# A two-layer mixture-of-experts encoder on one core: layer 1's gather in two float32r parts, and the sums of a block in halves at other places

## The chip, the core and the metric

The kernel runs on one core of a Trainium2 chip. Its engines are TensorE (PE, with its weight loads as PEld), VectorE (DVE), ScalarE (ACT), GpSimd (POOL) and SyncE (SP), which issues the loads from memory. The metric is the device time of one execution in microseconds; lower is better.

## What is computed

Two layers over 256 tokens of width 1024, each a token mixer (windowed attention, a state-space part and latent attention, joined by an output projection) followed by experts, and one normalisation at the end. The change lies in the experts. Each token picks one of 4 groups and 2 of its 8 experts (32 in all), each with matrices of 1024 x 256 (gate, up) and 256 x 1024 (down), all in float32:

```
for g in range(N_EXPERT_GROUPS):
    h = jax.nn.silu(jnp.einsum('nd,edf->enf', xt, w_gate[g])) * jnp.einsum('nd,edf->enf', xt, w_up[g])
    h = h * gate[:, g].T[:, :, None].astype(h.dtype)
    y = y + jnp.einsum('enf,efd->nd', h, w_down[g])
```

Only the tokens that chose an expert have a gate other than zero, and the kernel computes each expert for those alone.

## The kernel before

**Blocks.** `ORDER` (L26) puts the experts of a layer into nine blocks, of two experts with up to 64 token slots each or of four with 32. In layer 1 these are, in order: 16-17, 0-3, 18-19, 4-7, 8-11, 12-15, 20-23, 24-27, 28-31. Neighbouring blocks of equal size and consecutive experts form a group (L1206): in layer 1, 4-7 with 8-11 and 20-23 with 24-27; the others stand alone. A block has 128 slots, so a group has 128 or 256.

**Gather.** `onehot` (L1214) makes a 0/1 matrix `P` that takes tokens to the slots of a group, in two halves of 128 tokens. `gather` (L1232), for each of 8 slices `k` of the width, multiplies the normalised tokens `xn` (the stationary operand, 128 x 128) by `P` (moving, 128 or 256 columns), both halves of tokens into one bank, and ScalarE or VectorE in turn moves the result with the gain into the page `xe`. The first group is gathered at the layer's start, any other during the last block of the group before it, slices 0 to 3 and 4 to 7 apart (L1578 to L1585). `xn` is written by `normed` (L1175), a ScalarE copy of the tokens times their scale, at the end of the mixer (steps `r0` and `r1` of `SEQ`).

**A block** (from L1518): `fill_slots` turns the weighted one-hot into the combine matrix `Sm`; `gate_up` (L1440) multiplies the gathered slots by the gate and up weights, in two halves of the width; `hidden` (L1345) is a ScalarE silu and a VectorE product, `hidden_t` (L1351) two transposes and a copy; `down` (L1459) multiplies by the down weights, and `split_y` (L1359) splits the result into two float32r parts. `combine` (L1245) adds the block to the tokens `x`, for each half of the width and of the tokens by two float32r matmuls (L1251, L1252) and a VectorE addition (L1253). It is done late: the sums of a block are pending (`pend`) until the next block's gate products are through. The order in the program is: gate products of both halves; then for part 0 and 1: the next group's gather of that part, the pending sum of that part, and after part 0 the transposes of `hidden_t`; then an `If` (L1598) that all engines pass; then the down products.

```
for part in range(2):
    if ib == nb - 1 and nxt:
        for k in range(4 * part, 4 * part + 4):
            gather(nxt[0], nxt[1], k)
    if pend is not None:
        combine(pend, (part,))
    if part == 0:
        hT = hidden_t(hh)
```

**Overflow.** With more than 32 tokens for an expert of a block of four, `second` (L1489, under the `If`s of L1568 and L1598) repeats the block for the rest, with a gather of its own (`gather_all`, L1477); with more than 64 or 128, `unit` (L1381) does 128 slots of one expert, after the sixth block of layer 1 (`UNIT_AT`). Its gather (L1398) moves 512 columns of `xn`. In the profiled execution one unit and one `second` run, both in layer 1.

**Order on the engines.** The tile framework plans each engine's order at build time from the program order and from what its plan has ready; `pin` keeps a few in place. An `If` is planned as a unit.

**Loads.** Weights come in pages of 1 MB (128 x 8 KB) through one SP queue in the order of `chunks`. The ring has `NPAGE` = 25 pages, shared by weights and work pages. `room` (L211) lets a page in as long as weights and work pages fit, with `st["peak"]` pages kept for work; `done` and `work_done` free pages and call `pump` (L227), which issues the next loads. `KEEP` (L42), the pages `xe` and `xn`, is held from `r0` to the end of a layer's experts.

Of the kernel before, what the change touches and what calls it, by code (L numbers as in the profile page):

```python
# [41 lines left out]
KEEP = ("xe", "xn")  # L42
# [7 lines left out]
        "gl": ("ub", "qkv", "hT", "hTl"), "R": (), "r0": KEEP, "r1": KEEP, "e0": KEEP, "e1": KEEP, "h0": (), "h1": (), "k0": (), "k1": (),  # L50
# [111 lines left out]
def hybrid_encoder_kernel(ctx, tc, I, out, dbg=None):  # L162
# [48 lines left out]
    def room(key):  # L211
# [13 lines left out]
        return key in eat or len(KEEP) + sum(1 for k in st["tiles"] if k not in eat) < NPAGE  # L225
# [339 lines left out]
    def uses(l, w):  # L565
# [8 lines left out]
        if w in USES:  # L574
            u = list(USES[w])
        elif w[0] in "nq":
# [38 lines left out]
    def mixer(l):  # L615
# [68 lines left out]
        with tc.tile_pool(name=f"mx{l}", bufs=1, reuse_waits="tile") as mp:  # L684
# [413 lines left out]
            next(follow(l, SEQ[l].split() + ["|"], steps, KEEP))  # L1098
            st["plan"], st["peak"] = None, len(KEEP)
# [3 lines left out]
    class Router:  # L1103
# [22 lines left out]
        def pages(self):  # L1126

            self.xe = work["xe"]
            self.xT, self.xn = page_sm(self.xe, 0, (8, T)), page_sm(work["xn"], 0, (2, 8, 128))
            self.junk = self.xn[:, 1].rearrange("p k d -> p (k d)")  # L1130
# [44 lines left out]
        def normed(self, tt):  # L1175
            S.activation(self.xn[:, tt], self.xk[:, tt], AF.Copy, scale=self.r2[:, tt:tt + 1])
# [17 lines left out]
    def moe(l, tab, rt):  # L1194
        with tc.tile_pool(name=f"moe{l}", bufs=1, reuse_waits="tile") as mo:
# [4 lines left out]

            xe_pg, xn, msk, rk, gate = rt.xe, rt.xn, rt.msk, rt.rk, rt.gate
            io32 = iota[:, 0:NE]
            st["peak"] = len(KEEP)
# [21 lines left out]
            def weigh(P, ex):  # L1225
                shape = [128, 2] + list(P.shape[2:])
                pgt = mt(shape, "pgt")
                G.tensor_tensor(pgt, P,  # L1228
# [152 lines left out]
            def unit(u):  # L1381
# [7 lines left out]
                Pu, Pg = mt([128, 2, 128], "Pu", tag="oh"), page_sm(scr[0], 1536, (2, 128))  # L1389
# [99 lines left out]
            def second(blk, w, hf):  # L1489

                if hf == 0:
                    sh = [128, 2, 4, 32]
                    e0 = blk[0]
                    P, Pg = w["P"], scr[0][:, 1280:1536].rearrange("p (t e c) -> p t e c", t=2, e=4)
# [211 lines left out]
```

## Time and profile before

| | us |
|---|---|
| median of 3 runs (727.12 to 731.55) | 730.94 |
| the profiled execution, its own time | 735.1 |
| its span, first to last instruction | 733.3 |
| PE busy | 639.2 (87%) |
| DVE busy | 373.2 (51%) |
| ACT busy | 252.9 (34%) |
| POOL busy | 107.4 (15%) |
| read from memory | 233.82 MB, 320 GB/s over the span |

Busy time is the time in which an engine has an instruction under way; PE's is modelled and runs over the drain of a matmul. An f32 matmul leaves two records, a float32r matmul one. "DVEq L1598" is VectorE's sequencer at the `If` of that line.

### The profile page before, as it was taken

How to read it: one execution, taken by the hardware profiler on the slowest of the kernel's cores; microseconds unless marked ns; L12 is line 12 of the kernel's file. 1: busy time of each engine (PE TensorE's matmuls, PEld its weight loads, DVE VectorE, ACT ScalarE, POOL GpSimd, SP SyncE). 2: the span in 40 equal slices, each digit the busy share in tenths (PEclk: the TensorE clock that was granted, in tenths of full speed). 3: DMA queues.
4: the chain of work that ended last, by engine and by line, in shares of the span. 5: the costliest groups of instructions: out<-in, count | busy, mean ns of one | idle time of the engine just before them, and what ended most of it. 6: DMA issues, size and time to landing. Idle time of an engine off the chain costs nothing. (4 is left out here: it accounts for less than half of the span.)

```text
span 733.3 us, 12000 instructions
## 1 busy us (share of the span) xinstructions
PE 639.2 (87%) x4370; PEld 389.2 (53%) x4370; DVE 373.2 (51%) x899; ACT 252.9 (34%) x578; POOL 107.4 (15%) x135
## 2 busy tenths in 40 slices
PE   7997989988799797778899899999989978889994
PEld 6584877744245243326468777775534434334442
DVE  3899977532432228624369877762333323422424
ACT  3647764332111113444073397432202111011113
POOL 1202000100000022312032754500000000000001
PEclk9999999999899999789999899997999999999998
DMA  8920374895999999999996714796799999999991
GB/s 309 419 105 0 118 275 177 329 386 200 409 410 416 307 416 407 414 414 409 396 417 251 286 59 142 261 363 267 241 414 408 413 408 415 412 410 358 408 380 71
DMA packets 57201, 232.82 MB, mean 317 GB/s; under 512 B 6049, under 2 KB 8481, under 8 KB 48161
## 3 DMA queue, kind: packets, MB, share of 16 engines
q1 hardware_dynamic: 57120, 231.75, 81.3%
q8 instruction: 51, 0.84, 0.5%
q14 instruction: 30, 0.24, 0.1%
HBM read 233.82 MB, written 1.05 MB: 320 GB/s over the span
## 5 line engine op out<-in xcount | busy, mean ns | idle before, releaser
L1451 PE MATMUL gu<-pg,xe 128*32 128x512 f32 (+1 forms) x1024 | 149.5, 619 | 11.4 <-DMA pg<-in_w_up_dram 9.9
L1467 PE MATMUL yp<-pg,scr 128*32 128x512 f32 (+2 forms) x560 | 77.9, 628 | 26.1 <-DVEq L1598 12.8
L1451 PEld LDWEIGHTS gu<-pg,xe 128*32 128x32 f32 (+1 forms) x1024 | 45.9, 117 | 98.8 <-issue 94.5
L1236 PE MATMUL gp<-oh,xn 128*128 128x128 f32 (+1 forms) x416 | 73.6, 331 | 3.9 <-DVE oh L1221 1.6
L1236 PEld LDWEIGHTS gp<-oh,xn 128*128 128x128 f32 x416 | 62.9, 201 | 19.0 <-issue 11.3
L1467 PEld LDWEIGHTS yp<-pg,scr 128*32 128x32 f32 (+1 forms) x560 | 21.6, 119 | 72.1 <-issue 57.2
L1361 DVE TENSOR_TENSOR y<-yp,y 128x512 fp32r<-128x512 f32 (+1 forms) x39 | 26.3, 677 | 65.2 <-ACT y L1360 65.2
L1253 DVE TENSOR_TENSOR x<-cp,x 128x512 f32<-128x512 f32 x76 | 48.9, 684 | 19.0 <-PE cp L1252 19.0
L1228 POOL TENSOR_TENSOR pgt<-oh,gate 128x256 f32<-128x256 f32 (+1 forms) x13 | 10.2, 782 | 305.5 <-PE slp L372 294.3
L1348 DVE SCALAR_TENSOR_TENSOR scr<-gu,gs,scr 128x256 f32<-128x256 f32 x19 | 9.2, 482 | 89.9 <-ACT scr L1347 89.9
L1360 ACT CAST y<-yp 128x512 fp32r<-128x512 f32 (+1 forms) x39 | 22.3, 574 | 86.5 <-PE yp L1467 82.7
L359 DVE TENSOR_SCALAR xe<-gp,vec 128x128 f32<-128x128 f32 (+1 forms) x52 | 20.8, 400 | 54.6 <-PE gp L1236 54.6
L355 ACT ACTIVATE xe<-gp,vec 128x128 f32<-128x128 f32 (+1 forms) x52 | 21.1, 408 | 76.5 <-PE gp L1236 76.5
L1347 ACT ACTIVATE scr<-gu 128x256 f32<-128x256 f32 x19 | 7.3, 383 | 99.8 <-PEq L1568 50.9
L1251 PE MATMUL cp<-y,sm 128*128 128x512 f32 x76 | 33.5, 449 | 0.3 <-PEq L1568 0.2
L1252 PE MATMUL cp<-y,sm 128*128 128x512 f32 x76 | 29.9, 402 | 1.5 <-DVE y L1361 1.5
L1058 DVE SCALAR_TENSOR_TENSOR x<-op,rg,x 128x512 f32<-128x512 f32 x24 | 17.9, 748 | 16.9 <-PE op L681 11.9
L1341 ACT ACTIVATE scr<-slp 128x256 f32<-128x256 f32 x20 | 7.7, 387 | 35.4 <-PE slp L372 15.6
L1251 PEld LDWEIGHTS cp<-y,sm 128*128 128x128 f32 x76 | 14.3, 189 | 10.4 <-issue 8.2
L372 PE MATMUL hp<-cst,scr 128*128 128x128 f32 x40 | 9.2, 313 | 10.9 <-DVE scr L1348 9.8
L548 PE MATMUL t4p<-ca,tabs 128*32 128x32 f32 (+3 forms) x512 | 16.3, 250 | 2.1 <-issue 2.1
L548 PEld LDWEIGHTS t4p<-ca,tabs 128*32 128x32 f32 x512 | 15.4, 116 | 3.3 <-issue 3.0
(454 smaller groups left out, 1210.2 us busy)
## 6 DMA issues: line engine op xcount, KB each, us to landing
pg<-in_w_gate_dram SPq DMA_DIRECT2D x128, 512.0 KB, 10.2
pg<-in_w_up_dram SPq DMA_DIRECT2D x128, 512.0 KB, 10.2
pg<-in_w_down_dram SPq DMA_DIRECT2D x56, 1024.0 KB, 12.0
pg<-in_w_o_dram SPq DMA_DIRECT2D x8, 1024.0 KB, 17.9
pg<-in_w_down_dram SPq DMA_DIRECT2D x12, 512.0 KB, 10.4
pg<-in_w_qk_dram SPq DMA_DIRECT2D x4, 1024.0 KB, 14.9
pg<-in_w_nat_dram SPq DMA_DIRECT2D x4, 960.0 KB, 12.9
wgu<-in_w_gate_dram SPq DMA_DIRECT2D x4, 512.0 KB
```

The costliest lines, as they stand in the source:

```text
L355: S.copy(dst, src) if scale is None else S.activation(dst, src, AF.Copy, scale=scale)
L359: e.tensor_scalar(dst, src, scale, None, op0=OP.mult)
L548: PE.matmul(t4p[b][32 * jq:32 * jq + 32, c + lo:c + hi], g0[ri][:, 8 * d + i, :], ca[ri][:, 8 * d + i, m, :].rearrange("p m c -> p (m c)") ...
L1058: V.scalar_tensor_tensor(xh, p, rg[:, g, tt:tt + 1], xh, op0=OP.mult, op1=OP.add)
L1236: PE.matmul(p[:, :w], xn[:, tt, k, :], P[:, tt].rearrange("p e c -> p (e c)"), start=(tt == 0), stop=(tt == 1))
L1251: PE.matmul(p, Sm[:, 128 * tt:128 * tt + 128], yh[:, c], start=True, stop=False)
L1252: PE.matmul(p, Sm[:, 128 * tt:128 * tt + 128], yl[:, c], start=False, stop=True)
L1253: V.tensor_tensor(x[:, tt, c], p, x[:, tt, c], OP.add)
L1360: S.copy(yh[:, c], yp)
L1361: V.tensor_tensor(yl[:, c], yp, yh[:, c].bitcast(F32), OP.subtract)
L1451: PE.matmul(gu[m * s:m * s + m, :].rearrange("p (a f) -> p a f", a=2), xs(k, s), page(l, "gu", e, hf)[:, :, k % 4, :], start=(k == 0), sto ...
L1467: PE.matmul(yp[m * s:m * s + m, :], hT[:, j, m * s:m * s + m], page(l, "dn", e)[:, j, c], start=(j == 0), stop=(j == 1), tile_position=(0, ...
```

## The change

In layer 1 `xn` becomes two float32r pages: `xn`, the rounded value, and `xl`, the rest, which a VectorE instruction after ScalarE's copy computes. One-hots become float32r, and each gather product becomes two, with `xn` and with `xl`, into the same bank; so in `gather`, `gather_all` and the unit's gather. `KEEP` has a third page in layer 1, and the peaks count it. In layer 0 the gather stays as it is.

In both layers the pending sums move: the first half stands between the two halves of the gate products, the second after `hidden_t` and ahead of the gather's second part.

```
-KEEP = ("xe", "xn")
+KEEP = (("xe", "xn"), ("xe", "xn", "xl"))
...
+            self.xn = [page_sm(work[n], 0, (2, 8, 128)) for n in KEEP[self.l][1:]]
+            if self.l:
+                self.xn = [t.bitcast(F32R) for t in self.xn]
+            self.junk = self.xn[-1][:, 1].rearrange("p k d -> p (k d)")
...
         def normed(self, tt):
-            S.activation(self.xn[:, tt], self.xk[:, tt], AF.Copy, scale=self.r2[:, tt:tt + 1])
+            hi = self.xn[0][:, tt]
+            S.activation(hi, self.xk[:, tt], AF.Copy, scale=self.r2[:, tt:tt + 1])
+            if self.l:
+                V.scalar_tensor_tensor(self.xn[1][:, tt], self.xk[:, tt], self.r2[:, tt:tt + 1], hi.bitcast(F32),
+                                       op0=OP.mult, op1=OP.subtract)
...
+            one = F32R if l else F32
...
-                P = mt([128, 2, n, cap], "oh")
+                P = mt([128, 2, n, cap], "oh", one)
...
                 for tt in range(2):
-                    PE.matmul(p[:, :w], xn[:, tt, k, :], P[:, tt].rearrange("p e c -> p (e c)"),
-                              start=(tt == 0), stop=(tt == 1))
+                    for t in xn:
+                        PE.matmul(p[:, :w], t[:, tt, k, :], P[:, tt].rearrange("p e c -> p (e c)"),
+                                  start=(tt == 0 and t is xn[0]), stop=(tt == 1 and t is xn[-1]))
...
-                        PE.matmul(p, Pu[:, tt], xn[:, tt, 4 * hf:4 * hf + 4, :].rearrange("p k d -> p (k d)"),
-                                  start=(tt == 0), stop=(tt == 1))
+                        for t in xn:
+                            PE.matmul(p, Pu[:, tt], t[:, tt, 4 * hf:4 * hf + 4, :].rearrange("p k d -> p (k d)"),
+                                      start=(tt == 0 and t is xn[0]), stop=(tt == 1 and t is xn[-1]))
...
-                            PE.matmul(p[:, 128 * k:128 * k + 128], xn[:, tt, 4 * hf + k, :], P[:, tt],
-                                      start=(tt == 0), stop=(tt == 1))
+                            for t in xn:
+                                PE.matmul(p[:, 128 * k:128 * k + 128], t[:, tt, 4 * hf + k, :], P[:, tt],
+                                          start=(tt == 0 and t is xn[0]), stop=(tt == 1 and t is xn[-1]))
...
                             with tc.If(more > 0):
                                 second(blk, w, 0)
                             done(*[(l, "gu", e, 0) for e in blk])
+                            if pend is not None:
+                                combine(pend, (0,))
                             gate_up(gu, blk, xs, 1)
                     elif b > 0:
                         for hf in range(2):
+                            if hf and pend is not None:
+                                combine(pend, (0,))
                             gate_up(gu, blk, xs, hf)
                             done(*[(l, "gu", e, hf) for e in blk])
 
                     hh = hidden(gu, gs)
                     for part in range(2):
+                        if part == 1 and pend is not None:
+                            combine(pend, (1,))
                         if ib == nb - 1 and nxt:
                             for k in range(4 * part, 4 * part + 4):
                                 gather(nxt[0], nxt[1], k)
-                        if pend is not None:
-                            combine(pend, (part,))
                         if part == 0:
                             hT = hidden_t(hh)
...
-                        st["peak"] = 8
+                        st["peak"] = len(KEEP[l]) + 6
...
-                        st["peak"] = 4
+                        st["peak"] = len(KEEP[l]) + 2
```

## Rows read from the trace of the kernel before

**Rows 1.** Page, the span in 40 slices of 18.3 us: DMA share in tenths, GB/s.

```profile
DMA  8920374895999999999996714796799999999991
GB/s 309 419 105 0 118 275 177 329 386 200 409 410 416 307 416 407 414 414 409 396 417 251 286 59 142 261 363 267 241 414 408 413 408 415 412 410 358 408 380 71
```

**Rows 2.** Windows of layer 1's experts: length, busy time per engine (count), PEclk, DMA share, GB/s.

```profile
504.00:517.60 13.60, 13.60 (x88) 8.25 (x88) 4.85 (x15) 3.90 (x11) 0.61 (x1) 1.00 0.41 155
517.60:526.00 8.40, 8.25 (x66) 3.13 (x66) 1.12 (x2) 0.96 (x3) 0.62 (x1) 1.00 0.88 250
...
534.80:594.00 59.20, 54.61 (x374) 26.00 (x374) 20.01 (x38) 10.73 (x27) 1.66 (x2) 1.00 1.02 412
...
661.50:717.00 55.50, 51.15 (x390) 24.74 (x390) 17.74 (x34) 9.27 (x24) 0.62 (x1) 1.00 1.00 374
```

**Rows 3.** Timeline of SP, the loads: start us, us, engine, line, what.

```profile
491.37 12.99 SPq L247 DMA_DIRECT2D pg<-in_w_down_dram  x2
504.45 0.39 SPq L247 DMA_DIRECT2D pg<-in_w_gate_dram  x1
...
517.58 0.34 SPq L247 DMA_DIRECT2D pg<-in_w_gate_dram  x1
```

**Rows 4.** Waits of PE, 517 to 625 us: total us, times, longest.

```profile
PE gu L1451 <- DMA pg<-in_w_up_dram: 2.4, 2, 1.5
...
PE yp L1467 <- DMA pg<-in_w_down_dram: 1.5, 1, 1.5
```

**Rows 5.** Waits of PE, 625 to 725 us.

```profile
PE yp L1467 <- DVEq L1598: 2.4, 2, 1.2
```

**Rows 6.** Timeline of PE: start us, us, shapes, how many, [idle before].

```profile
487.67 3.66 PE L1146 MATMUL lp<-pg,xe 128*128 128x40 f32 x32
...
606.11 3.69 PE L1236 MATMUL gp<-oh,xn 128*128 128x256 f32 x16
...
619.84 3.62 PE L1467 MATMUL yp<-pg,scr 128*32 128x512 f32 x26 [1.46 <-DMA pg<-in_w_down_dram]
...
629.10 5.23 PE L1398 MATMUL gpu<-xn,Pu 128*128 128x512 f32 x8 [2.85 <-DVE Pu L1391]
...
661.71 3.81 PE L1483 MATMUL gpa<-scr,xn 128*128 128x128 f32 x32 [0.24 <-DVE scr L1495]
...
723.11 0.28 PE L1265 MATMUL cp<-y,sm 128*128 128x256 f32 x1
723.22 0.28 PE L1266 MATMUL cp<-y,sm 128*128 128x256 f32 x1
723.39 0.50 PE L1265 MATMUL cp<-y,sm 128*128 128x256 f32 x2
```

**Rows 7.** Weight loads: by shape (mean ns after the busy time), and one in the timeline.

```profile
L1236 PEld LDWEIGHTS gp<-oh,xn 128*128 128x128 f32 x416 | 62.9, 201 | 19.0 <-issue 11.3 <-ACT dv L1186 3.5
...
L1251 PEld LDWEIGHTS cp<-y,sm 128*128 128x128 f32 x76 | 14.3, 189 | 10.4 <-issue 8.2 <-ACTq L1427 0.2
...
494.95 0.15 PEld L1172 LDWEIGHTS <-tri 128*128 128x128 bf16 x1
```

**Rows 8.** Windows of the router's end and of the unit's gather.

```profile
489.60:496.20 6.60, 4.01 (x27) 3.54 (x26) 4.89 (x32) 5.63 (x10) 0.74 (x2) 0.70 0.97 350
...
629.00:634.30 5.30, 5.20 (x10) 2.36 (x11) 1.35 (x4) 0.00 (x0) 0.00 (x0) 0.69 1.03 410
```

**Rows 9.** ScalarE's copy in the timeline, and a group of the page.

```profile
492.49 2.16 ACT L1176 ACTIVATE xn<-x,r 128x1024 f32<-128x1024 f32 x1 [0.95 <-POOL r L341]
...
L1058 DVE SCALAR_TENSOR_TENSOR x<-op,rg,x 128x512 f32<-128x512 f32 x24 | 17.9, 748 | 16.9 <-PE op L681 11.9
```

**Rows 10.** Timeline of the ninth block of layer 1.

```profile
714.92 2.47 DVE L1253 TENSOR_TENSOR x<-cp,x 128x512 f32<-128x512 f32 x4
...
715.06 0.51 PE L372 MATMUL hp<-cst,scr 128*128 128x128 f32 x2
...
717.71 2.79 PE L1467 MATMUL yp<-pg,scr 128*32 128x512 f32 x32 [1.20 <-DVEq L1598]
```

More of the change, by code (lines that the diff above doesn't have):

```diff
@@ L224, in room @@
                 return False
-        return key in eat or len(KEEP) + sum(1 for k in st["tiles"] if k not in eat) < NPAGE
+        return key in eat or len(KEEP[key[0]]) + sum(1 for k in st["tiles"] if k not in eat) < NPAGE
     def pump(limit=None):
@@ L575, in uses @@
             u = list(USES[w])
+        elif w in ("r0", "r1", "e0", "e1"):
+            u = list(KEEP[l])
         elif w[0] in "nq":
@@ L1097, in mixer @@
             st["plan"] = plans[l]
-            next(follow(l, SEQ[l].split() + ["|"], steps, KEEP))
-            st["plan"], st["peak"] = None, len(KEEP)
+            next(follow(l, SEQ[l].split() + ["|"], steps, KEEP[l]))
+            st["plan"], st["peak"] = None, len(KEEP[l])
             return held["rt"]
@@ L1128, in pages @@
             self.xe = work["xe"]
[L1129 to L1130 removed]
+            self.xT = page_sm(self.xe, 0, (8, T))
+            self.xn = [page_sm(work[n], 0, (2, 8, 128)) for n in KEEP[self.l][1:]]
+            if self.l:
+                self.xn = [t.bitcast(F32R) for t in self.xn]
+            self.junk = self.xn[-1][:, 1].rearrange("p k d -> p (k d)")
         def tokens(self, tt):
@@ L1199, in mt @@
                 return mo.tile(shape, dt, tag=tag or name, name=name, bufs=bufs)
+            one = F32R if l else F32
             xe_pg, xn, msk, rk, gate = rt.xe, rt.xn, rt.msk, rt.rk, rt.gate
             io32 = iota[:, 0:NE]
-            st["peak"] = len(KEEP)
+            st["peak"] = len(KEEP[l])
             blks = blocks(l)
@@ L1227, in weigh @@
                 pgt = mt(shape, "pgt")
-                G.tensor_tensor(pgt, P,
+                G.tensor_tensor(pgt, P.bitcast(F32),
                                 gate[:, :, ex[0]:ex[0] + len(ex)].unsqueeze(3).to_broadcast(shape), OP.mult)
@@ L1388, in unit @@
                 V.tensor_scalar(rs_[:, 0:2], rs_[:, 0:2], ub[:, MAXU + u:MAXU + u + 1], None, op0=OP.subtract)
-                Pu, Pg = mt([128, 2, 128], "Pu", tag="oh"), page_sm(scr[0], 1536, (2, 128))
+                Pu, Pg = mt([128, 2, 128], "Pu", one, tag="oh"), page_sm(scr[0], 1536, (2, 128))
                 for tt in range(2):
@@ L1493, in second @@
                     e0 = blk[0]
-                    P, Pg = w["P"], scr[0][:, 1280:1536].rearrange("p (t e c) -> p t e c", t=2, e=4)
+                    P = (w["S"][0] if l else scr[0][:, 1024:1280]).rearrange("p (t e c) -> p t e c", t=2, e=4)
+                    Pg = scr[0][:, 1280:1536].rearrange("p (t e c) -> p t e c", t=2, e=4)
                     V.tensor_tensor(P, iota[:, 33:65].unsqueeze(1).unsqueeze(1).to_broadcast(sh),
                                     rk[:, :, e0:e0 + 4].unsqueeze(3).to_broadcast(sh), OP.is_equal)
-                    V.tensor_tensor(Pg, P, gate[:, :, e0:e0 + 4].unsqueeze(3).to_broadcast(sh), OP.mult)
+                    V.tensor_tensor(Pg, P.bitcast(F32), gate[:, :, e0:e0 + 4].unsqueeze(3).to_broadcast(sh), OP.mult)
                     gather_all(P.rearrange("p t e c -> p t (e c)"), w["xs"])
@@ L1604, in moe @@
                     if b == 0:
-                        st["peak"] = 4
+                        st["peak"] = len(KEEP[l]) + 2
                     if b != UNIT_AT[l]:
@@ L1615, in moe @@
                         units(nc.values_load(uw["ui"][0:1, n:n + 1], min_val=0, max_val=MAXU))
-                        work_done(6, 4)
+                        work_done(6, len(KEEP[l]) + 2)
                     if b >= TAB_AT and tab is not None:
@@ L1623, in moe @@
                 combine(pend)
-            for n in KEEP:
+            for n in KEEP[l]:
                 del work[n]
-            work_done(len(KEEP) + 1)
+            work_done(len(KEEP[l]) + 1)
     plans = [make_plan(l) for l in range(L)]
@@ L1639, in hybrid_encoder_kernel @@
         nc.sync.dma_start(x[:, 1, :], I["x"][128:256, :])
-        work.update((n, work_page(n)) for n in KEEP)
+        work.update((n, work_page(n)) for n in KEEP[0])
         pump()
```

2 lines of the change are left out of this document (removed), and 1 row of the table USES.

## The prediction

> **What bounds the kernel now.** I read the slices first. The DMA line [rows 1] is full in two long stretches, each the expert part of a layer, and thin in between; the forecast depends on which stretches are full and who ends them. The windows view cuts layer 1's expert part into pieces [rows 2]: from 504 to 517.6 us the DMA share is 0.41 while PE is busy 13.60 of 13.60 us; from 534.8 to 594 it is 1.02 at 412 GB/s while PE has 4.6 us of gaps; from 661.5 to 717 PE is busy 51.2 of 55.5 us. SP's timeline says why the first piece is thin [rows 3]: the ring is full, a load goes out at 491.37, the next when the first experts' pages come free at 504, and the stream starts in earnest at 517.58, when the down products of the first block end. From there the loads set the pace. The waits of PE between 517 and 625 [rows 4] show it: 2.4 us on gate/up pages and 1.5 us on a down page, the latter the last (PE goes on at 619.84 with the sixth block's down products [rows 6]). In the same view from 625 on [rows 5] PE waits for no DMA; it waits for other engines, such as 2.4 us in two waits for VectorE to reach the `If` of L1598.
>
> So layer 1's end is a chain of three parts. PE up to 517.6 decides when loading restarts; loading decides the moment of 619.84; PE decides the rest. What PE saves between 517.6 and 619.84 only lengthens its waits. Layer 0's expert part has the same form, with a full DMA line up to its last page, and no gather changes there.
>
> **Part 1, the gather of layer 1 in two parts.** A gather product now is an f32 matmul, recorded as two records; it becomes two float32r matmuls, one record each. Seven groups are gathered, five 128 slots wide and two 256 wide. What counts is the pitch from one start to the next. Half a 256-wide f32 group issues 16 records from 606.11 on in 3.69 us; without the 0.4 us that the last one takes to drain that is 0.21 us a record. A float32r matmul over 256 columns starts 0.11 us after the one before it (723.11, 723.22) [rows 6]. So a 256-wide group goes from 32 x 0.21 = 6.7 us to 32 x 0.11 = 3.5 us, both groups together 6.4 us less. They are gathered in the third and the sixth block, the latter at 606 to 614 us, inside the stretch that loading sets: worth nothing at the end.
>
> For 128 columns no float32r row exists. The f32 record there has a pitch of 0.11 us (32 in 3.81 us at 661.71), and so have f32 products that move only 40 columns: 32 records in 3.66 us [rows 6]. With so little to move, that is the pitch of loading 128 f32 weights, not of moving columns. The load records of float32r (L1251, 189 ns) and f32 (L1236, 201 ns) are alike [rows 7], so I take 0.11 us a record: 32 records before and after, no change. The bounds: 0.055 us, if the load took half as long, and 0.22 us, if a narrow float32r product took the passes of a whole f32 product. That is 1.75 us less or 3.5 us more for each 128-wide group.
>
> [...]
>
> The `units` path of layer 1 runs once, after 620, on PE's part of the chain. [...] The one executed overflow gather, L1483 at 661.71, has 32 records, 128 wide: unchanged at 0.11.
>
> **Part 2, the low parts.** Two VectorE instructions over 1024 elements are added ahead of the first gather, and they need ScalarE's copies, which take 2.16 us each on the same strided operand [rows 9]. The nearest VectorE row has 512 elements in 748 ns, so one takes 1.4 us, and 2.16 at most. Between 489.6 and 496.2 VectorE is busy 4.89 of 6.6 us [rows 8] with the routing chain that ends in the one-hots of L1221, for which PE waits. 4.89 + 2.8 = 7.7 us, 1.1 more than there is; with 4.3 it would be 2.6, with perfect overlap 0. I take **+1.1 us**, all of it ahead of 517.6 and so on the path.
>
> **Part 3, the page.** `xl` holds a ring page from `r0` of layer 1 to the end. At 484 to 504 the ring is full [rows 3], so one page fewer is loaded ahead; the pages freed afterwards are as many as before, and loading stays one page behind when it is full. A page is 1.05 MB, at 412 GB/s [rows 2] **+2.55 us** at 619.84. Zero is possible only if some later gap takes it up; before 620 I see none. After 625 it is hidden, since PE waits for no page there [rows 5].
>
> **Part 4, the sums.** Nothing is added: four product pairs and four VectorE additions per block move ahead, one half before the second gate products, the other before the gather's second half. Where a gather follows, the last additions leave VectorE before the gather's last evictions, so the `If` comes sooner. After 620 that is the eighth block alone: its 1.2 us wait should shrink to some 0.7, **-0.5 us** (bounds 0 and -1.2). In the ninth block there is no gather. Before: additions from 714.92 on, the transpose at 715.06, down products at 717.71 [rows 10]. The first half used to cover the wait for `hidden`; moved ahead, 1.05 us of PE is spent earlier and that wait lies open. If the second half is issued into the gap the sum is 0, if not it is +1.05. I take 0: the planner does put what is ready first, as the two L1265 in a row at 723.39 show [rows 6]. The seventh block has nothing pending after `units`. In layer 0 and in layer 1 before 620 the moves meet slack from loading: 0. Pages of the summed `y` come free sooner, which helps nothing while loading is full.
>
> **Sum**: 1.1 + 2.55 - 1.7 - 0.5 = +1.45 us. The profiled execution has a span of 733.3 and its own time is 735.1, 4.2 us above the median 730.94. On its scale the span becomes 734.75; on the median's **732.4 us**. One per cent, 7.3 us, is about what a measurement of this kernel tells from no change.
>
> **Rivals.**
> - *Narrow float32r is slow* (0.22 us a record at 128 columns). For: every float32r product in the trace moves 256 columns or more, so nothing excludes it. [...] Price: the two gathers of the first block add 7.0 us ahead of 517.6, and all loading follows; those of the second and the fifth are paid by the 6.4 us of the 256-wide ones and by PE's waits; the eighth block's gather and the overflow gather add 3.5 each after 620. 1.45 + 14.0 = +15.45: **746.4 us**, slower by 2.1%. It decides from about 0.16 us a record on, where 4 x 32 records cost 5.9 us more.
> - *The weights load faster* (0.055). The same four gathers with the opposite sign, 1.75 each: 1.45 - 7.0 = -5.55: **725.4 us**. For: a shorter bf16 load. Against: the 189 ns. [...]
> - *Page and low parts are hidden*: VectorE fits both instructions into the chain's latencies, and the missing page is made up for because PE frees pages sooner between 517.6 and 530. For: the DMA share is 0.88 at the start of that [rows 2], so there is room. 1.45 - 3.65: **728.7 us**.
> - *The moves do nothing*, because the planner restores the old order: 0.5 us, inside the forecast's own range.
>
> **How the numbers follow.** The forecast gets 0.48, slow narrow products 0.28, hidden page 0.12, faster loads 0.12. The forecast's own range is 729 to 736 (low parts 0 to 2.6, unit 0 to 3.4, ninth block up to +1.05). With the rivals the range is 724 to 748; it leaves out the far ends of the fast and the slow case. Faster by over 1% (under 723.6): half of the faster loads and a remainder, 0.10. Slower by over 1% (over 738.2): the slow case and the forecast's tail, 0.31. Within 1%: 0.59.
>
> **What would show it.** Right: L1236 in layer 1 still has 224 records, now 32 in some 3.5 us whatever the width; one page fewer goes out before the first block's pages come free; the low parts stand on VectorE near 490 to 497 and the first gate product starts about 1 us later; the sixth block's last down page lands 3 to 4 us later and PE waits for it longer than 1.5 us; L1398 takes 3.4 us. Wrong: 128-wide records at 0.2 us or at 0.06 us; PE not waiting for the sixth block's pages at all; the ninth block's products starting over 4.5 us after its gate products' end.

## The result

The change made the kernel slower: 739.0 us against 730.77 us (medians of 20 runs each), ratio 1.0118 with a 95% interval of 1.0096 to 1.0141, or 8.2 us by the medians. That is inside the range of the forecast (724 to 748), 6.6 us above its number, and outside its likeliest class, since 1.2% is just over the 1% that was to count as no change. The forecast's own range ended at 736; the wider one reached to 748 for narrow float32r products of 0.22 us, which did not come about, so that the result lies inside it by luck. The profiled execution of after took 737.75 us with a span of 736.0; before it was 735.1 and 733.3.

The slices of after, as [rows 1]:

```profile
DMA  8920375896999999999993516983999999999981
GB/s 316 420 94 0 117 299 211 335 386 232 415 406 416 345 414 414 410 413 406 400 419 146 229 58 224 323 311 115 349 414 410 411 411 413 415 372 407 408 311 58
```

The hole ahead of layer 1's full stretch is deeper: its last three slices read 311, 115 and 349 GB/s, where before they read 363, 267 and 241, and then 414 in both.

The two executions differ by 5.6 us ahead of layer 1's router for reasons of their own, so all that follows counts from the start of the first product of layer 1's router logits: 487.67 before [rows 6], 482.10 after. This is PE's timeline of after, in the order in which rows 6 stand (start us, us, shapes, how many, idle before):

```profile
482.10 3.66 PE L1152 MATMUL lp<-pg,xe 128*128 128x40 f32 x32
...
496.51 5.21 PE L1464 MATMUL gu<-pg,xe 128*64 128x512 f32 x16
...
502.06 0.28 PE L1248 MATMUL gp<-oh,xn 128*128 128x128 f32 x1
502.17 0.28 PE L1248 MATMUL gp<-oh,xl 128*128 128x128 f32 x1
...
542.67 0.28 PE L1248 MATMUL gp<-oh,xl 128*128 128x256 f32 x1
542.79 0.28 PE L1248 MATMUL gp<-oh,xn 128*128 128x256 f32 x1
...
619.65 5.05 PE L1480 MATMUL yp<-pg,scr 128*32 128x512 f32 x26 [1.47 <-DMA pg<-in_w_down_dram]
...
630.32 0.77 PE L1411 MATMUL gpu<-xn,Pu 128*128 128x512 f32 x1 [2.85 <-DVE Pu L1403]
...
633.87 1.99 PE L372 MATMUL xup<-cst,xu 128*128 128x128 f32 x8
```

The float32r products of 128 columns start 0.11 us apart (502.06, 502.17), those of 256 columns 0.12 us (542.67, 542.79), both at a granted clock of 1.00. The layer's first gather runs at a lower clock, 0.50 from 492.79 to 496.51; its products start 0.21 us apart, as the f32 records of before do in the same place and at the same clock (eight in 2.05 us at 493.32). The matmuls themselves are as forecast. The first gate product starts at 496.51, 14.41 us after the logits; before it was 10.56. The rows of VectorE, ScalarE and GpSimd in between say why:

```profile
482.84 2.15 ACT L1183 ACTIVATE xn<-x,r 128x1024 fp32r<-128x1024 f32 x1
...
485.02 2.07 DVE L1185 SCALAR_TENSOR_TENSOR xl<-x,r,xn 128x1024 fp32r<-128x1024 f32 x1 [0.20 <-ACT xn L1183]
...
486.11 0.98 POOL L340 TENSOR_SCALAR r<-ssq 128x1 f32<-128x1 f32 x1 [3.99 <-ACT xl L1141]
...
487.01 0.15 DVE L1163 TENSOR_TENSOR pen<-cst,gi 128x4 f32<-128x4 f32 x1
...
487.76 2.14 ACT L1183 ACTIVATE xn<-x,r 128x1024 fp32r<-128x1024 f32 x1 [1.74 <-POOL r L341]
...
489.93 2.05 DVE L1185 SCALAR_TENSOR_TENSOR xl<-x,r,xn 128x1024 fp32r<-128x1024 f32 x1 [0.72 <-ACT xn L1183]
...
491.90 0.18 DVE L1167 MAX8 e<-em 128x8 f32<-128x32 f32 x1
...
492.36 0.28 DVE L1232 TENSOR_TENSOR oh<-cst,rk 128x128 fp32r<-128x128 f32 x1
...
492.79 0.45 PE L1248 MATMUL gp<-oh,xn 128*128 128x128 f32 x1 [3.31 <-DVE mk L1169]
```

The first low part (485.02, 2.07 us) stands in VectorE's order ahead of L1163 of the first half's routing, which so begins at 487.01, and the second (489.93, 2.05 us) ahead of L1167, L1179 and the one-hot L1232 at 492.36, for which PE waits; its first gather product is at 492.79. While the first low part runs, GpSimd's L340, a scale of one column, takes 0.98 us; it puts off `r`, ScalarE's second copy (487.76) and with it the second low part.

The loads of SP in after, as [rows 3]:

```profile
485.79 0.33 SPq L247 DMA_DIRECT2D pg<-in_w_gate_dram  x1
...
501.75 0.80 SPq L247 DMA_DIRECT2D pg<-in_w_down_dram  x2
515.13 0.34 SPq L247 DMA_DIRECT2D pg<-in_w_gate_dram  x1
```

One page goes out at 485.79, two at 501.75, and the next at 515.13, when the first block's down products end. Counted to the end of the kernel, 80 pages are still to be issued when the stream restarts at 515.13, where before had 79 at 517.58: the one page of the forecast. Then the waits of PE, 515 to 625 us and 625 to 727 us, as [rows 4, 5]:

```profile
PE gu L1464 <- DMA pg<-in_w_up_dram: 5.2, 4, 1.6
PE yp L1480 <- DMA pg<-in_w_down_dram: 2.9, 2, 1.5
...
PE yp L1480 <- DMA pg<-in_w_gate_dram: 1.2, 1, 1.2
...
PE hp L372 <- DVE scr L1360: 3.1, 3, 1.1
...
PE yp L1480 <- DVEq L1616: 1.2, 1, 1.2
```

PE waits 5.2 us for gate and up pages, 2.9 for down pages, and 1.2 for a wait put down to a gate page, where before had 2.4 and 1.5; loading still decides when the sixth block's down products go on, at 619.65 or 137.55 us after the logits, where before it was 619.84 or 132.17 [rows 6]. After that a wait shows that before did not have in the ninth block, `hp` for VectorE's `hidden` (L1360). Its timeline, as [rows 10]:

```profile
715.14 0.48 DVE L1360 SCALAR_TENSOR_TENSOR scr<-gu,gs,scr 128x256 f32<-128x256 f32 x1 [4.91 <-ACT scr L1359]
...
715.68 0.51 PE L372 MATMUL hp<-cst,scr 128*128 128x128 f32 x2 [1.00 <-DVE scr L1360]
...
715.94 0.48 PE L1263 MATMUL cp<-y,sm 128*128 128x512 f32 x1
...
718.29 4.38 PE L1480 MATMUL yp<-pg,scr 128*32 128x512 f32 x32 [1.17 <-DVEq L1616]
```

The sums' second half (715.94) stands behind the transpose `hp`, not in the gap ahead of it, so PE idles 1.00 us at 715.68 and again 1.17 us at 718.29 (before: 1.20), and the down products that follow take 4.38 us where before took 2.79. The windows show the clock there and in the sixth block (columns as in rows 2):

```profile
587.83:624.70 36.87, 27.98 (x142) 10.44 (x141) 6.52 (x12) 4.10 (x10) 1.05 (x1) 0.86 1.02 412
714.68:725.00 10.32, 8.15 (x59) 3.30 (x59) 4.03 (x7) 2.18 (x5) 0.42 (x1) 0.83 0.04 13
```

The granted clock is 0.86 in the sixth block, in which PE waits for pages, and 0.83 from the ninth block's gate products' end on; before it was 1.00 in both stretches.

### The profile page after: what moved, and what is told of

Its sections match the earlier page's. It is cut to its first block, busy times and chain, and to the rows that moved or that the text cites. A ratio compares the mean times of both kernels' runs of the same rounds, so it can differ in the third digit from the quotient of the medians.

```text
span 736.0 us, 12007 instructions
## 1 busy us (share of the span) xinstructions
PE 637.1 (87%) x4370; PEld 381.6 (52%) x4370; DVE 379.1 (52%) x901; ACT 252.8 (34%) x578; POOL 108.7 (15%) x135
## 3 DMA queue, kind: packets, MB, share of 16 engines
HBM read 233.82 MB, written 1.05 MB: 319 GB/s over the span
## 5 line engine op out<-in xcount | busy, mean ns | idle before, releaser
L1464 PE MATMUL gu<-pg,xe 128*32 128x512 f32 (+1 forms) x1024 | 156.3, 630 | 12.4 <-DMA pg<-in_w_up_dram 12.1
L1464 PEld LDWEIGHTS gu<-pg,xe 128*32 128x32 f32 (+1 forms) x1024 | 42.4, 118 | 106.3 <-issue 99.3
L1248 PE MATMUL gp<-oh,xn 128*128 128x128 f32 (+1 forms) x304 | 63.9, 320 | 4.0 <-DVE mk L1169 3.3
L1373 DVE TENSOR_TENSOR y<-yp,y 128x512 fp32r<-128x512 f32 (+1 forms) x39 | 26.2, 676 | 69.7 <-ACT y L1372 69.7
L1248 PEld LDWEIGHTS gp<-oh,xn 128*128 128x128 f32 x304 | 53.6, 200 | 13.1 <-ACT dv L1196 5.8
L1360 DVE SCALAR_TENSOR_TENSOR scr<-gu,gs,scr 128x256 f32<-128x256 f32 x19 | 9.1, 480 | 76.9 <-ACT scr L1359 76.9
L1248 PE MATMUL gp<-oh,xl 128*128 128x128 f32 (+1 forms) x112 | 28.9, 296 | 0.0
L1060 DVE SCALAR_TENSOR_TENSOR x<-op,rg,x 128x512 f32<-128x512 f32 x24 | 17.9, 748 | 16.8 <-PE op L683 11.9
L1248 PEld LDWEIGHTS gp<-oh,xl 128*128 128x128 f32 x112 | 23.6, 210 | 0.4
L372 PE MATMUL hp<-cst,scr 128*128 128x128 f32 x40 | 9.5, 319 | 14.8 <-DVE scr L1360 13.7
L1353 ACT ACTIVATE scr<-slp 128x256 f32<-128x256 f32 x20 | 7.7, 387 | 33.4 <-PE slp L372 19.4
```

Of the source, the lines that this page charges most:

```text
L1060: V.scalar_tensor_tensor(xh, p, rg[:, g, tt:tt + 1], xh, op0=OP.mult, op1=OP.add)
L1248: PE.matmul(p[:, :w], t[:, tt, k, :], P[:, tt].rearrange("p e c -> p (e c)"), start=(tt == 0 and t is xn[0]), stop=(tt == 1 and t is xn[-1]))
L1373: V.tensor_tensor(yl[:, c], yp, yh[:, c].bitcast(F32), OP.subtract)
L1464: PE.matmul(gu[m * s:m * s + m, :].rearrange("p (a f) -> p a f", a=2), xs(k, s), page(l, "gu", e, hf)[:, :, k % 4, :], start=(k == 0), sto ...
```

## Where the 8 us are

This table is worked out from PE's timelines, one execution per kernel: differences between the start of the router's logits, of first gate products, of the sixth block's down products behind the last wait for a page, and the ends of down products.

| kernel | logits to first gate product | to PE going on after the last wait for a page | to end of 6th block's down | 6th to 8th block's down | 8th to 9th block's down | logits to 9th block's down |
|---|---|---|---|---|---|---|
| before | 10.56 | 132.17 | 135.79 | 80.18 | 19.19 | 235.16 |
| before, again | 10.54 | 132.33 | 135.95 | 79.53 | 19.19 | 234.67 |
| after | 14.41 | 137.55 | 142.60 | 78.41 | 21.89 | 242.90 |
| after, again | 14.41 | 138.02 | 143.25 | 78.56 | 21.92 | 243.73 |
| page alone | 10.65 | 132.85 | 136.47 | 80.03 | 19.05 | 235.55 |
| after without low parts | 10.87 | 132.09 | 138.61 | 75.86 | 20.31 | 234.78 |
| gather, old sums | 14.43 | 137.91 | 143.03 | 79.20 | 19.06 | 241.29 |
| moves alone | 10.55 | 132.60 | 136.22 | 79.59 | 20.74 | 236.55 |
| moves, layer 0 | 10.60 | 133.35 | 138.43 | 79.67 | 19.19 | 237.29 |
| moves, layer 1 but 9th | 10.56 | 133.37 | 136.99 | 79.47 | 19.20 | 235.66 |
| moves, 8th block | 10.59 | 132.69 | 136.30 | 78.44 | 19.20 | 233.94 |
| after, 9th block old | 14.41 | 137.87 | 143.09 | 78.56 | 19.05 | 240.70 |
| one part | 9.60 | 128.22 | 133.54 | 73.29 | 19.04 | 225.87 |

Between the means of the two executions of before and of after, the loading part lost 7.1 us, the stretch from the sixth to the eighth block gained 1.4, the ninth block lost 2.7: 8.4 us in all, close to the 8.2 of the medians. Of the 7.1 us, 5.5 are loading: after its last wait for a page PE goes on at 137.8 us instead of 132.3. The other 1.5 are TensorE's clock: the down products behind that wait took 5.05 and 5.23 us in after, the first at a granted clock of 0.71, the second by the ratio of the times at an estimated 0.69, and 3.62 us at 1.00 in before.

In the column of that wait the kernels fall into two groups: 137.6 to 138.0 us with the low parts, 132.1 to 133.4 without them (128.2 with one part), whether the page is kept and the sums are moved or not. The stream restarts at 33.0 to 33.4 us after the logits with 80 pages left in the four executions with low parts, and at 28.4 to 30.0 us (one part: 26.2) with 79 left in all the others. So 3.7 of the 5.5 us are there at the restart, and the other 1.8 go with the one page more.

In the next column the clock is mixed in. In seven of these executions the products behind the last wait took 5.05 to 6.52 us, which against the 3.62 us at 1.00 of before gives estimated clocks of 0.55 to 0.71; PE had waited twice for down pages just before, 1.03 us or more each time. In the other six they took 3.62 us, after at most one wait that long. So two kernels with the same layer 1 stand 2.6 us apart there (135.79 and 138.43), 1.2 of it loading and 1.5 the clock, and a single execution can't settle anything smaller in this column. The others repeat within a few tenths where the clock is the same.

## Experiments on the gather

**The page alone.** The kernel before, with one more page reserved in layer 1 and not used; the peaks and the pages that are freed follow `KEEP` as in the change.

```diff
-KEEP = ("xe", "xn")
+KEEP = (("xe", "xn"), ("xe", "xn", "xl"))
...
```

> The kernel before with a third page of the ring held through layer 1 and not used; nothing else. Theory: one page fewer is loaded ahead of the first block, and the sixth block's last down page lands 2.55 us later: +2.55 us, ratio 1.0035 (1.002 to 1.006). Rival 1, the page is hidden because PE frees pages sooner later on: 0 us, ratio 1.000. Rival 2, the longer wait also lowers PE's clock and costs twice: +5 us, ratio 1.007.

Measured: 732.43 us, ratio 1.0032 (1.0011 to 1.0053), 2.3 us. The loads of SP:

```profile
489.86 11.54 SPq L247 DMA_DIRECT2D pg<-in_w_down_dram  x2
506.79 0.34 SPq L247 DMA_DIRECT2D pg<-in_w_gate_dram  x1
...
514.63 0.33 SPq L247 DMA_DIRECT2D pg<-in_w_gate_dram  x1
```

Counted from the logits, a page goes out at 21.0 us (506.79) that before had sent at 16.8 (504.45), and the stream restarts at 28.8 (514.63) with 79 pages left, as in before: by then the page is made up. The price is the forecast's, and both rivals lie outside the interval, but this one trace doesn't show where it is paid. PE goes on after its last wait for a page at 132.85 us, where before it was 132.17 and 132.33, and at a clock of 1.00.

**No low parts.** The kernel after without L1185; the gather takes the high part twice, so the gathered rows are twice the rounded ones.

```diff
-            if self.l:
-                V.scalar_tensor_tensor(self.xn[1][:, tt], self.xk[:, tt], self.r2[:, tt:tt + 1], hi.bitcast(F32),
-                                       op0=OP.mult, op1=OP.subtract)
...
-            xe_pg, xn, msk, rk, gate = rt.xe, rt.xn, rt.msk, rt.rk, rt.gate
+            xe_pg, xn, msk, rk, gate = rt.xe, [rt.xn[0][:, :] for _ in rt.xn], rt.msk, rt.rk, rt.gate
```

> The kernel after without the two low parts on VectorE: the second part of the gather reads the high part again, so that the gathered values are wrong, and matmuls, page and moves stay as they are. Theory: the low parts stand in the middle of VectorE's routing chain and put off the first gate product by 3.9 us, all loading of layer 1 with it: 3.9 us less than after, +4.3 us over before, ratio 1.006 (1.003 to 1.008), first gate product 10.5 to 11 us after the router's logits. Rival 1, my forecast's size: 1.1 us less than after, ratio 1.0095. Rival 2, the page alone decides when the loads come and the low parts are hidden behind it: ratio 1.011, as after.

Measured: 732.02 us, ratio 1.0025 (0.9997 to 1.0053). Against after's 1.0118 that is 0.93% or 6.8 us for two VectorE instructions, more than the theory's 3.9; the rivals, 1.1 us and none, are refuted. From its timeline:

```profile
486.42 2.16 ACT L1183 ACTIVATE xn<-x,r 128x1024 fp32r<-128x1024 f32 x1
...
489.70 0.19 POOL L340 TENSOR_SCALAR r<-ssq 128x1 f32<-128x1 f32 x1 [4.00 <-ACT xl L1141]
...
490.56 2.20 ACT L1183 ACTIVATE xn<-x,r 128x1024 fp32r<-128x1024 f32 x1 [0.95 <-POOL r L341]
...
491.39 1.51 PE L1245 MATMUL gp<-oh,xn 128*128 128x128 f32 x6 [1.30 <-DVE gi L1162]
...
617.77 6.52 PE L1477 MATMUL yp<-pg,scr 128*32 128x512 f32 x26 [1.47 <-DMA pg<-in_w_down_dram]
```

L340 takes 0.19 us again, the second copy starts 4.88 us after the logits (after: 5.66), and the first gather product 5.71 us after them, where after needed 10.69. The first gate product is 3.5 us sooner than in after, and PE goes on after its last wait for a page (617.77) at 132.09 us, 5.7 us sooner than in the mean of after's two executions and as soon as in before. The third page is kept here, but 79 pages are left when the stream restarts, not 80 as in after. The sixth block's down products end only 4.3 us sooner, because the products behind that wait take 6.52 us here: the granted clock is 0.50 from 617.68 to 621.68, and some 0.55 over all of them by the ratio to 3.62 us at 1.00. Of the 2.6 us that it gains in the stretch behind, 1.7 are the clock's: the seventh block's gate products, the same in both, take 18.73 us at 1.00 where after took 20.43 at 0.92. Whether the low parts bring that lower clock about isn't shown: the kernels without low parts have it too (before: 20.69 us at 0.92).

**Neighbouring elements.** The low part and ScalarE's copy read `x` with a step of eight elements. Here both parts are kept in the input's order, and PE reads the weights with that step instead.

```diff
-            S.activation(hi, self.xk[:, tt], AF.Copy, scale=self.r2[:, tt:tt + 1])
+                hi, lo = (t[:, tt].rearrange("p k d -> p (k d)") for t in self.xn)
+                S.activation(hi, x[:, tt, :], AF.Copy, scale=self.r2[:, tt:tt + 1])
...
+                xn = [t.rearrange("p t k d -> p t (k d)").rearrange("p t (d k) -> p t k d", k=8) for t in xn]
```

> The kernel after with both parts of the normalised rows kept in the order of the input, so that ScalarE's copies and VectorE's low parts read and write neighbouring elements, and TensorE reads the parts with a step of eight elements as weights. Theory: the step of the operands makes the low part last 2.05 us; without it it lasts some 1.3 us (a subtraction over 512 neighbouring elements takes 0.68 us here), the copy less too, and the first gate product comes at least 1.5 us sooner after the router's logits than in the kernel after (14.4 us): ratio to before 1.009 (1.006 to 1.011). Rival 1, the step isn't what costs: the low part lasts 2.05 us, ratio 1.012. Rival 2, loading weights with a step is slower than 0.11 us a record: the first block's gather of 64 records grows, ratio 1.014 or more.

Measured: 764.92 us, ratio 1.0491 (1.0459 to 1.0524). Copy and low part in its timeline, and two products of the gather:

```profile
481.73 1.15 ACT L1187 ACTIVATE xn<-x,r 128x1024 fp32r<-128x1024 f32 x1
...
483.63 1.27 DVE L1188 SCALAR_TENSOR_TENSOR xl<-x,r,xn 128x1024 fp32r<-128x1024 f32 x1
...
499.81 0.40 PE L1253 MATMUL gp<-oh,xn 128*128 128x128 f32 x1
500.05 0.40 PE L1253 MATMUL gp<-oh,xl 128*128 128x128 f32 x1
```

The copy takes 1.15 us where it took 2.15, the low part 1.27 where it took 2.07, and the first gate product comes 12.2 us after the logits: the theory's half of the price, and the step is what makes the instructions long. The second rival took all of it back and more: the products start 0.24 us apart instead of 0.11. The weight loads say why, first in this kernel, then in after:

```profile
L1253 PEld LDWEIGHTS gp<-oh,xl 128*128 128x128 f32 x112 | 37.7, 337 | 0.2
```

```profile
L1248 PEld LDWEIGHTS gp<-oh,xl 128*128 128x128 f32 x112 | 23.6, 210 | 0.4
```

337 ns a load with the step, 210 without. Of the two kernels, the one in which ScalarE and VectorE read with the step, once for each row, is the faster.

**Gather without the moves.** The kernel after with `combine` in both layers put back to its old places.

> The kernel after with the sums of both layers put back to their old places: gather in two parts, low parts and page remain. Theory: 8.2 less the 2.0 us of the moves, +6.2 us over before, ratio 1.0085 (1.006 to 1.011); PE's first gate product of layer 1 comes 14.4 us after the router's logits, as in the kernel after. Rival A (the moves carry the loss): +3 us or less, ratio under 1.004. Rival B (the moves gain in layer 0): +11 us, ratio 1.015.

Measured: 736.95 us, ratio 1.0103 (1.0063 to 1.0142), 7.5 us. The theory's 6.2 and the first gate product (14.43 us) hold, and both rivals lie outside the interval.

## Experiments on the sums

**The moves alone**, **in layer 0 alone**, and **in layer 1 without its ninth block**: the kernel before with these lines, in the first case without the conditions.

```diff
+                            if l == 0 and pend is not None:
+                                combine(pend, (0,))
                             gate_up(gu, blk, xs, 1)
...
+                        if l == 0 and part == 1 and pend is not None:
+                            combine(pend, (1,))
                         if ib == nb - 1 and nxt:
...
-                        if pend is not None:
+                        if l and pend is not None:
                             combine(pend, (part,))
```

> The kernel before with the moves of the sums alone, in both layers; gather and pages as before. Theory: the 8.2 us of the change come from the low parts (some 3.9 us), the page (2.55 us) and the clock that falls while PE waits; the moves cost only what the ninth block shows, 1.1 us of open wait and 1.6 us of slower down products at the end, less the 0.7 us of the eighth block: +2.0 us, ratio 1.003 (0.999 to 1.005). Rival A, the moves carry the loss, since the sums now stand ahead of gate products in all blocks of both layers: +5 us or more, ratio 1.007 or above. Rival B, the moves gain in layer 0, whose expert part ended 5.5 us earlier in the profile after: -3 us, ratio 0.996 or less.

> The kernel before with the moves of the sums in layer 0 alone. Theory: layer 0's expert part ends when its last pages land, and the moves meet slack: no change, ratio 1.000 (0.997 to 1.003). Rival: the kernel with the moves in both layers came out 1.007, of which its trace shows only 1.4 us in layer 1; the rest, some 3 us, is layer 0's: ratio 1.004 or above.

> The kernel before with the moves of the sums in layer 1 alone, without its ninth block. Theory: only the eighth block's wait for the branch is after the last wait for loading, and it shrinks by 0.7 us, as in the traces of the two kernels that have all moves: ratio 0.999 (0.996 to 1.002). Rival, the sums put off the gate products of the blocks before and with them the loads: +3 us, ratio 1.004 or above.

Measured: 733.61 us and 1.007 (1.004 to 1.010) for both layers; 732.26 us and 1.0038 (1.0014 to 1.0061) for layer 0; 733.08 us and 1.0042 (1.0015 to 1.0069) for layer 1 without the ninth block. The theory was too low each time, and the numbers came out as rival A and the two rivals of the single layers had them: the moves are not free in layer 0, and not a gain in layer 1. Rival B fell. But the sizes don't add up: by the ratios the gather without the moves costs 7.5 us, the moves alone 5.1, and both together 8.6. Beside the gather the moves cost 1.1 us (1.0118 against 1.0103), which the intervals can't tell from nothing. So what the moves cost within the change isn't shown by the timing. The ninth blocks of both layers show a part of what they cost alone. PE in layer 1's ninth block, moves alone:

```profile
713.49 0.50 PE L372 MATMUL hp<-cst,scr 128*128 128x128 f32 x2 [1.00 <-DVE scr L1348]
...
716.11 2.79 PE L1467 MATMUL yp<-pg,scr 128*32 128x512 f32 x32 [1.17 <-DVEq L1602]
```

The wait at `hp` is after's, 1.00 us, but the down products take 2.79 us as before, at a clock of 1.00. From the eighth block's to the ninth block's down products it is 1.5 us more than before. PE in layer 0's ninth block, first with the moves there, then in the second execution of the kernel before:

```profile
361.29 0.51 PE L372 MATMUL hp<-cst,scr 128*128 128x128 f32 x2 [1.01 <-DVE scr L1348]
...
363.89 3.64 PE L1467 MATMUL yp<-pg,scr 128*32 128x512 f32 x32 [1.16 <-DMA pg<-in_w_u_dram]
```

```profile
359.39 0.50 PE L372 MATMUL hp<-cst,scr 128*128 128x128 f32 x2
...
362.03 3.55 PE L1467 MATMUL yp<-pg,scr 128*32 128x512 f32 x22 [1.20 <-DVEq L1598]
```

There is the same 1.01 us of open wait, and the down products start 227.4 us after layer 0's logits. The two executions of before have 225.5 (shown) and 228.1, so one pair doesn't settle it; over the seven executions without moves there the mean is 225.2 us, over the seven with them 227.5. In the kernel before the second half of these products waits only 0.3 us for a page, so loading hides no more than that of the delay. From the eighth to the ninth block's down products of layer 0 the seven profiles without moves there take 29.4 to 30.8 us (mean 29.9), the seven with them 29.3 to 33.6 (mean 31.4). That is some 1.5 of the 2.8 us; the rest, and most of the 1.0042 of layer 1, I can't place: its sixth block ends 1.1 us later than before, which is inside that column's scatter.

**The eighth block alone, the kernel before again, the kernel after again.** The first puts the two conditions to `l and b == 7`.

> The kernel before with the sums moved in layer 1's eighth block alone. Theory: from its first gate product to its first down product it takes 13.6 instead of 14.3 us, and nothing else changes: 0.7 us less, ratio 0.999 (0.996 to 1.002). Rival: moves in other blocks than those cost the 3 us of the last run with moves in layer 1, and this one gives 0.7 us as well, but the second run of the kernel before shows that such ratios move by 0.003 without any change; then none of them can be read below 0.4 per cent.

> The kernel before once more, unchanged. Theory: its executions differ ahead of layer 1's router (in the ten profiles so far the logits start at 481 to 488 us) and by a page's time of loading after it, and the comparison gives 1.000 (0.997 to 1.003); from the router's logits to the last record of PE it takes 235 to 239 us again. Rival: the profile I read was a slow one in layer 1 as well, and this one takes 234 us or less; then the 1.004 of the two kernels with some of the moves are real there.

> The kernel after once more, unchanged. Theory: ratio 1.012 (1.009 to 1.014); the first gate product 14.4 us after the router's logits, the sixth block's down products end at 142 to 143.5 us, the ninth block waits 1 us for its hidden values; whether the clock falls in the ninth block is chance, so that from the logits to the last record it takes 242 to 245 us. Rival: the clock falls there each time, 244.5 us or more.

Measured: 0.9989 (0.9965 to 1.0013) for the eighth block; 1.0007 (0.9980 to 1.0034) for before against itself; 1.0114 (1.0068 to 1.0161) for after. From the eighth block's first gate product to its first down product it takes 13.7 us instead of 14.3, as expected, and the timing can't tell 0.7 us. The kernel before measured against itself gave 1.0007, with an interval of 0.3% to each side, so the 1.0038 and 1.0042 are small but above what no change gave. The rival for before fell: from the logits to the last record of PE it took 236.45 us, the first time 236.95. For after the rival held: I had called the low clock in the ninth block chance, but it came again, and to the last record it took 245.5 us, where 242 to 245 were expected:

```profile
722.27 0.50 PE L372 MATMUL hp<-cst,scr 128*128 128x128 f32 x2 [1.00 <-DVE scr L1360]
...
724.88 4.40 PE L1480 MATMUL yp<-pg,scr 128*32 128x512 f32 x32 [1.17 <-DVEq L1616]
```

With after's order of the ninth block the down products took 4.4 us in both executions of after and 2.8 us in the moves-alone kernel and in after without low parts, with the same waits ahead of them. What decides between them stays open.

**After, with the ninth block's sums in their old place.**

```diff
+                    last = end and b == len(blks) - 1
...
-                            if pend is not None:
+                            if pend is not None and not last:
                                 combine(pend, (0,))
...
+                        if pend is not None and last:
+                            combine(pend, (part,))
                         if part == 0:
                             hT = hidden_t(hh)
```

> The kernel after with the sums of layer 1's ninth block alone put back to their old place; nothing else. Theory: from the ninth block's first gate product to the last record of its down products it took 18.9 us before, 20.4 with the moves alone and 21.6 in the kernel after, where the clock fell as well; back in the old order it takes 18.8 us, 2.8 us less than after: ratio to before 1.008 (1.005 to 1.010). Rival 1, only the open wait goes and the clock stays low: 1.1 us less, ratio 1.010. Rival 2, the ninth block's order makes no difference to the end: ratio 1.012.

Measured: 739.89 us, ratio 1.0120 (1.0076 to 1.0164) from six runs, an interval of 3.2 us to each side. The trace shows the 2.8 us (19.05 against 21.9 us from the eighth to the ninth block's down products); the timing neither confirms nor excludes them.

## A version faster than both

If the narrow products cost 0.11 us whatever the type, then the second part, the low parts and the page are what the change pays for, and the halved count is what it could have had. The kernel before with the rows rounded to float32r, the change's types for the gather, and the low part left out (two places of it):

```diff
+                self.xn = [t.bitcast(F32R) for t in self.xn]
...
-KEEP = ("xe", "xn")
+KEEP = (("xe", "xn"), ("xe", "xn"))
```

> The kernel before with layer 1's gather in one float32r part: the rows are rounded to float32r and the low part is left out, so no low parts, no third page, and half the records; the sums stay in their old places. Theory: at 0.11 us a record the first block's two gathers lose 16 records or 1.75 us each, ahead of the restart of loading, and after the last wait for loading the second gather and the eighth block's lose 1.75 us each and the unit's gather, 4 records instead of 8 at either clock, 2.5 us: 3.5 + 6 us less than before, ratio 0.987 (0.983 to 0.991). Rival, what is saved ahead of the last wait for loading is lost there, since the stream is full anyway: 6 us less, ratio 0.992.

Measured: 725.42 us, ratio 0.9921 (0.9891 to 0.9951), 5 to 6 us faster than before and some 14 than after. It leaves out what the second part carried, so it is a choice of precision and not the same computation. From PE's timeline:

```profile
494.82 1.11 PE L1245 MATMUL gp<-oh,xn 128*128 128x128 f32 x8
...
619.17 2.04 PE L1408 MATMUL gpu<-xn,Pu 128*128 128x512 f32 x4 [2.85 <-DVE Pu L1400]
...
647.22 2.00 PE L1494 MATMUL gpa<-sm,xn 128*128 128x128 f32 x16
```

Eight products in 1.11 us at 494.82 where before issued sixteen records in 2.05 (at 504.06), four in the unit's gather (2.04 us against 5.23), sixteen in the second gather (2.00 us against 3.81). The trace shows both parts of the theory, 2.3 us ahead of the sixth block's end and 6.7 us behind it, 9.0 us in all. PE goes on after its last wait for a page 4.0 us sooner than in before, near the theory's 3.5, but 1.7 us of that are lost right behind it, where the down products take 5.32 us for 3.62 at a clock of 1.00 in before, an estimated 0.68 by the ratio. That execution was its fastest (718.14 us); the timing fits the rival's 6 us, so how much of the first part comes through in most executions isn't settled.

## Why the forecast was off, point by point

- **Pitch.** Right. 0.11 us at 128 columns and a clock of 1.00, no gain and no loss; the two rivals of 0.22 and 0.055 us, together 0.40 of the chances, fell by the first row. The loads measured 210 ns for `xl` in the gather (200 for `xn`, with layer 0's f32 loads among them) and 192 in the second gather, beside 201 before [rows 7]. Loads of float32r were no shorter than those of f32 here.
- **Low parts: +1.1, at most 2.6.** This is the step that failed. Against the kernel without them they put the first gate product off by 3.5 us, and the moment at which PE goes on after its last wait for a page by 5.7. Two things were wrong. The duration was taken from a row with neighbouring elements (L1058, 748 ns for 512), though the row beside it, ScalarE's 2.16 us on the same operand, was already the better measure [rows 9]: 2.07 us measured. And busy time was summed against the window's length, as if VectorE could do its work in any order. In the trace it works in the order issued: each low part stood ahead of a chain of short instructions that were ready, so its whole duration went on the chain. L1163 and L1167, whose operands were there at 484.82 and 489.09, began at 487.01 and 491.90. PE's first gather product came 5.0 us later than before (10.69 against 5.65 us after the logits), of which the two low parts are 4.1 and GpSimd's longer L340 0.8. The first gate product came 3.85 us later, because before's gather had waited in its middle as well.
- **Page: +2.55.** Right in size when timed alone, 2.3 us. Its place is not shown: the prediction saw no gap before 620 that could take it up, but in that trace and in after without low parts the page is made up ahead of the restart. Only with the low parts are 80 pages left there against 79.
- **Unit's gather: -1.7.** No run shows this term, its bounds or the 3.4 us for L1398. The eight products took 3.55 us (630.32 to 633.87) at a granted clock of 0.50, where before took 5.07 (0.50 up to 632 and 1.00 from 633 on), -1.5. But the transposes behind them took 2.22 us to the unit's gate products where before took 1.54, at a granted clock of 0.50 over the whole stretch; before it had risen on the way (0.76). That gave 0.7 us back. With the eighth block's share, the gain from the sixth to the eighth block's end was 1.4 us.
- **Eighth block: -0.5.** It was -0.7 in the traces: the wait for the branch shrank from 1.17 to 0.50 us.
- **Ninth block: 0, at most +1.05.** Failed. I expected the sums' second half in the gap ahead of `hp`, because two ready products had been put together elsewhere [rows 6]. The order is fixed before the run and put `hp` first, so the gap stayed empty: +1.1 to +1.5 us, about the bound, and 1.6 us more where the clock fell, which the bound left out. This is read from the traces; the timing with the old order of the ninth block did not show it.
- **Layer 0: 0.** Failed, by some 2.8 us when timed alone. Its ninth block shows some 1.5 of them: it has the same open wait, and the slack from loading there was 0.3 us.
- **Sum.** In the traces layer 1 lost 8.4 us where the sum had 1.45. At the last wait for a page it lost 5.5 for 3.65 (low parts and page), 1.9 more. The lower clock behind that wait, for which the sum had no term, is 1.5. From there to the eighth block's end it gained 1.4 for 2.2, 0.8 less, and the ninth block lost 2.7 for 0. That is 6.9 us, beside 6.6 between the forecast and the median. The 2.8 us of layer 0 find no place in it.

## What to carry to other kernels

Before a new instruction is put on an engine, look for what stands behind it in that engine's order, not for free time in a window: on a dependent chain its whole duration counts, here 2.07 and 2.05 us. Take its price from a row with the same access pattern; a step of eight elements made it 1.6 to 1.9 times as long here on all three engines that read it. And work that is moved away from a wait uncovers that wait, here 1.00 us: ask what else PE has to do there, in the last block above all, where no gather follows.

## What was not expected of the hardware

A step of eight float32 elements (32 bytes) costs ScalarE 2.15 us against 1.15, VectorE 2.07 against 1.27, and a weight load 337 ns against 210.

A GpSimd instruction of 0.19 us took 0.98 us beside the first low part on VectorE, and both ended at 487.09. In the kernel with neighbouring elements it took 0.94 us beside the shorter low part; it ended at 484.94 and the low part at 484.90. What ties the two together isn't shown.

float32r was no faster here below 256 columns: 0.11 us a record at 128 and 0.12 at 256, at a granted clock of 1.00; at 0.50 it was 0.21 at 128. That the weight loads set this pace is an inference: f32 products that move only 40 columns have 0.11 us as well at a clock of 1.00 [rows 6], and with loads of 337 ns the products start 0.24 us apart, in layer 1's first gather (489.94, 490.18) and in the next (499.81, 500.05) alike.
